# Modulation of layer 0 in float32 in four strips of the array, two parts ahead, and tokens in eight parts instead of five

## The chip, the core and the metric

The kernel runs on one core of one Trainium2 chip. The metric is the device time of one execution in microseconds; a version is judged by the median of several executions. Every time below is in microseconds unless marked ns.

## What is computed

Two blocks over 256 tokens of width 2048. The part that the change touches is the beginning of the first block, layer 0, which reads two sequences: the tokens x and a context ctx, each of 256 rows.

```python
def modulation(cond, w, b, n):
    m = jax.nn.silu(cond) @ w[:, :n * D_MODEL] + b[:n * D_MODEL]
    return jnp.split(m, n, axis=-1)

# layer 0 of first_block
sh, sc, gt = modulation(c_lat, w_ada[i], b_ada[i], 3)
u = x * (1.0 + sc) + sh
sh_c, sc_c = modulation(c_c, w_ada[i], b_ada[i], 2)
uc = ctx_s * (1.0 + sc_c) + sh_c
s_f, s_b = context_states(uc @ w_in_e[j][:, :E_STATE_COLS], ...)
y, _, _ = even_mixer(u @ w_in_e[j], s_f, s_b, ...)
x = layer_norm(alpha * x + gt * y, ln_g[i], ln_b[i])
```

The modulation is a product of two vectors (silu of c and of c_ctx, 2048 long) with the columns of w_ada: 2048 of the shift (kind 0), 2048 of the scale (kind 1) and, for x alone, 2048 of the gate. Its result is needed as one number for each of the 2048 channels. The matrix is 2048 x 6144 in float32 for a layer, 50 MB, and every element of it is used once for each of the two vectors.

The second block (a recurrent mixer, sparse attention, attention over a memory of 256 rows, an MLP) matters here only in that the keys and values of its memory are computed first of all.

## The kernel before

Everything is float32. A large product is done as three passes in a narrower format (called fp32r in the rows): both operands are split into a high and a low part, and `mm3` (L163 to L165) issues high x high, high x low and low x high into the same PSUM bank. The token side is split once, the weights as they come: `load_w` loads a tile "wr" of two k-tiles of 512 columns (512 KB, four buffers), `split_w` casts it to "wh" on ScalarE (L148) and subtracts on VectorE to get "wl" (L154, in two halves; three buffers each). A k-tile is 128 of the 2048 channels.

The work is written in order of program, and a planner (the tile framework) gives each engine its queue in an order by priority. Small streams of work that have to run beside a large one are written as generators: `bg[0]` holds one, `step(n)` advances it by n items at the places where it is called, and `drain()` runs it to its end.

The order of work around the change:

- **Memory stage** (0 to about 76 us). The memory is transposed into memT; `project` multiplies it with the 1024 columns of w_kv_cross_2, in two blocks of 512 columns with eight loads each. Beside it, one step a load, runs `ada_both(0)`, the modulation of k-tiles 0 and 1, and the norm of the memory.
- **Token stage** (to about 320 us). The loop over `PARTS`, five parts of 2, 2, 4, 4 and 4 k-tiles. A part loads its columns of x and ctx ("xn"), transposes them on TensorE (L236), applies scale and shift from mod0 and splits the result into high and low. Then, for four blocks of 512 columns of w_in_e, it loads the weights of its k-tiles and issues 24 products for each load (two k-tiles, four row blocks, three passes), into four PSUM banks. A bank is then added on VectorE to kl, vl, kc or vc (L555); in the first part it is copied by ScalarE instead.
- **Modulation for the next part** runs as `bg[0]` within the products of a part. Parts 1 and 2 get theirs from `ada_both`, two k-tiles and both kinds at a time: two loads of 256 KB into the two halves of one "wr", the same split as for any weight, and four products with c4, which holds high and low of both vectors in four columns (L349 and L350). For parts 3 and 4 kind 0 comes from `ada_block` in the same way (L327 and L328), and kind 1 from `ada_block_v` on VectorE alone: one multiply-add per k-tile and vector (L381), from the tile "ar" with two buffers. In each case a small selection product "pm" (L334, L356, L387) turns the result into one number per partition and channel, and a last VectorE instruction adds the bias into mod0. `drain()` at a part's end finishes what is left.
- **Gates and layer 1.** During the last part `bg[0]` becomes `gt_mod()`: the four gate blocks of layer 0 and the modulation of layer 1, 192 steps of one load "ar" of 256 KB and one VectorE multiply-add into "aa" (L403, L405), two steps a load of weights. The rest runs beside the stages that follow (chunked attention states up to about 865 us).

Of the kernel before, what the change touches and what calls it, by code (L numbers as in the profile page):

```python
# [8 lines left out]
F = mybir.dt.float32  # L9
# [8 lines left out]
D = 2048  # L18
# [36 lines left out]
def tile_kernel(ctx: ExitStack, tc: tile.TileContext, I: dict, out: bass.AP):  # L55
# [7 lines left out]
    PHASES = {"a": {"g": (1024, 12), "h": (512, 6), "f": (512, 6), "gt": (512, 4), "ar": (512, 2), "aa": (512, 1)},  # L63
# [245 lines left out]
    c4 = const([128, 16, 4], "c4", R)  # L309
    for a in range(2):  # L310
        col = cs[:, a * 16:(a + 1) * 16]
        S.copy(c4[:, :, 2 * a], col)
        V.tensor_tensor(c4[:, :, 2 * a + 1], col, c4[:, :, 2 * a].bitcast(F), op=AL.subtract)
    sel4 = cst[0:4, C_SEL4:C_SEL4 + 2]
# [4 lines left out]
    def ada_block(t0, nt, kind):  # L319

        n = nt * 128
        acc = pbg([4, n], "ada")
        nk = 1024 // n
        for k0 in range(0, 16, nk):
            wh, wl = load_w(ada[0], k0, nk, kind * D + t0 * 128, n)
            for q in range(nk):
                PE.matmul(acc, c4[:, k0 + q], wh[:, q], start=k0 + q == 0, stop=False)  # L327
                PE.matmul(acc, c4[:, k0 + q], wl[:, q], start=False, stop=k0 + q == 15)  # L328
            yield
        m4 = tl("h", [4, n], name="m4")  # L330
        V.tensor_copy(m4, acc)
        pm = pside([128, nt, 64, 2], name="pm")
        for q in range(nt):
            PE.matmul(pm[:, q], m4[:, q * 128:(q + 1) * 128], sel4[:, None, :].to_broadcast([4, 64, 2]), start=True, stop=True)  # L334
        for a in range(2):
            set_mod0(pm[:, :, 0, a], t0, nt, kind, a)

    def ada_both(t0):

        acc = pbg([4, 512], "ada")  # L340
        for k0 in range(0, 16, 2):
            wr = sb.tile([128, 2, 512], F, name="wr", tag="wr", bufs=4)
            for kind in range(2):
                c0 = kind * D + t0 * 128
                nc.sync.dma_start(wr[:, :, kind * 256:kind * 256 + 256],
                                  ada[0][k0 * 128:(k0 + 2) * 128, c0:c0 + 256].rearrange("(k p) m -> p k m", p=128))
# [8 lines left out]
        for q in range(4):  # L355
            PE.matmul(pm[:, q], m4[:, q * 128:(q + 1) * 128], sel4[:, None, :].to_broadcast([4, 64, 2]), start=True, stop=True)  # L356
# [1556 lines left out]
```

## Time and profile before

| what | value |
|---|---|
| median of three executions | 2561.5 us (2560.05 to 2563.88) |
| the profiled execution, its own time | 2557.92 us |
| its span on the chip | 2556.2 us |
| PE (TensorE products) busy | 2422.8 us, 95% |
| DVE (VectorE) busy | 1796.2 us, 70% |
| ACT (ScalarE) busy | 1170.2 us, 46% |
| POOL (GpSimd) busy | 172.1 us, 7% |
| granted TensorE clock, mean | 0.984 of full |
| DMA, mean | 189 GB/s; 483.11 MB in all |

The span runs from the first to the last instruction; the execution's own time contains 1.7 us more. Busy shares are means over all stages. Products on PE are pipelined and their durations overlap, so the time of a product is better read from the distance between two starts. "PEld" is the loading of weights into the array, which runs beside the products. The stationary operand of a product stands after the comma in its name, with its shape as rows x columns.

### The profile page before, as it was taken

How to read it: one execution, taken by the hardware profiler on the slowest of the kernel's cores; microseconds unless marked ns; L12 is line 12 of the kernel's file. 1: busy time of each engine (PE TensorE's matmuls, PEld its weight loads, DVE VectorE, ACT ScalarE, POOL GpSimd, SP SyncE). 2: the span in 40 equal slices, each digit the busy share in tenths (PEclk: the TensorE clock that was granted, in tenths of full speed). 3: DMA queues.
4: the chain of work that ended last, by engine and by line, in shares of the span. 5: the costliest groups of instructions: out<-in, count | busy, mean ns of one | idle time of the engine just before them, and what ended most of it. 6: DMA issues, size and time to landing. Idle time of an engine off the chain costs nothing.

```text
span 2556.2 us, 32427 instructions
## 1 busy us (share of the span) xinstructions
PE 2422.8 (95%) x11491; PEld 1928.6 (75%) x11491; DVE 1796.2 (70%) x2991; ACT 1170.2 (46%) x1560; POOL 172.1 (7%) x169
## 2 busy tenths in 40 slices
PE   8999998889989998998999999999999999999998
PEld 5667766778767776787878677787888888888886
DVE  5898657997897888967687978755655544555544
ACT  6543244444653544445642452445544433444433
POOL 0000010220230010002020120100000000000000
PEclk9999999999999999999999999999999999999999
DMA  7877547676656788755633243145466555666554
GB/s 262 276 251 225 170 153 242 218 232 228 198 183 218 233 282 288 259 182 158 198 94 110 80 136 99 63 163 192 133 189 182 186 187 187 189 184 187 201 188 154
DMA packets 267358, 483.11 MB, mean 189 GB/s; under 512 B 21137, under 2 KB 45547, under 8 KB 267195
## 3 DMA queue, kind: packets, MB, share of 16 engines
q1 hardware_dynamic: 266875, 480.60, 58.4%
q8 instruction: 90, 1.47, 0.2%
q14 instruction: 73, 0.60, 0.1%
q10 hardware_dynamic: 320, 0.44, 0.1%
HBM read 477.82 MB, written 3.15 MB: 188 GB/s over the span
## 4 chain that ended last, share of the span: by engine, by line
PE 61%; DVE 18%; DMA 11%; issue 6%; ACT 3%; POOL 1%; SPq 0%; DVEq 0%; ACTq 0%; POOLq 0%
PE acc L165 17%; PE acc L164 17%; PE acc L163 17%; DMA ar<-in_w_ada 8%; DVE wl L154 6%; DVE aa L405 3%; PE trp L236 2%; ACT wh L148 1%; DMA lnb<-in_ln_b 1%; PE pw L1457 1%; PE pz L1451 1%; DVE u L1411 1%; DVE inv L1412 1%; DMA wr<-in_w_in_e 1%; DMA wr<-in_w_in_o 0%
## 5 line engine op out<-in xcount | busy, mean ns | idle before, releaser
L148 ACT CAST wh<-wr 128x1024 fp32r<-128x1024 f32 (+2 forms) x736 | 760.3, 1038 | 991.6 <-PE acc L165 804.6
L164 PE MATMUL acc<-wl,xh 128*128 128x512 f32 (+2 forms) x2560 | 1005.5, 393 | 22.9 <-DVE wl L154 22.7
L163 PE MATMUL acc<-wh,xh 128*128 128x512 f32 (+2 forms) x2560 | 1011.8, 396 | 14.1 <-ACT xh L253 6.1
L165 PE MATMUL acc<-wh,xl 128*128 128x512 f32 (+2 forms) x2560 | 1003.5, 393 | 2.4 <-DVE xl L254 1.9
L154 DVE TENSOR_TENSOR wl<-wr,wh 128x512 fp32r<-128x512 f32 (+2 forms) x928 | 622.3, 702 | 176.8 <-ACT wh L148 176.1
L164 PEld LDWEIGHTS acc<-wl,xh 128*128 128x128 f32 x2560 | 485.1, 189 | 135.8 <-DVE wl L154 37.2
L151 DVE TENSOR_TENSOR wl<-wr,wh 128x1024 fp32r<-128x1024 f32 x272 | 333.3, 1225 | 357.4 <-ACT wh L148 355.4
L163 PEld LDWEIGHTS acc<-wh,xh 128*128 128x128 f32 x2560 | 484.6, 189 | 127.1 <-ACT wh L148 10.0
L165 PEld LDWEIGHTS acc<-wh,xl 128*128 128x128 f32 x2560 | 484.8, 189 | 106.3 <-issue 4.0
L405 DVE SCALAR_TENSOR_TENSOR aa<-ar,cs,aa 128x512 f32<-128x512 f32 x240 | 191.0, 796 | 72.8 <-DMA ar<-in_w_ada 71.5
L165 PE MATMUL acc<-wh,ucl 128*128 128x512 f32 x128 | 50.9, 398 | 0.0
L164 PE MATMUL acc<-wl,uch 128*128 128x512 f32 x128 | 50.7, 396 | 0.0
L163 PE MATMUL acc<-wh,uch 128*128 128x512 f32 x128 | 49.8, 389 | 0.0
L381 DVE SCALAR_TENSOR_TENSOR am<-ar,cs,am 128x512 f32<-128x512 f32 x60 | 42.6, 746 | 7.3 <-DMA ar<-in_w_ada 7.3
L722 PE MATMUL pp<-eq,ek 128*128 128x128 f32 x224 | 29.4, 286 | 6.1 <-DVE ek L734 6.1
L722 PEld LDWEIGHTS pp<-eq,ek 128*128 128x128 f32 x224 | 28.5, 201 | 8.4 <-issue 5.0
L1055 POOL TENSOR_TENSOR sgo<-sgo,psc 128x512 f32<-128x512 f32 x8 | 14.6, 1850 | 295.5 <-ACT sgo L1049 164.8
L350 PE MATMUL ada<-wl,c 128*4 128x512 f32 x64 | 26.0, 406 | 4.2 <-DVE wl L154 4.2
L164 PE MATMUL acc<-wl,dh 128*128 128x512 f32 x64 | 26.2, 410 | 3.8 <-DVE wl L154 3.7
L457 DVE SCALAR_TENSOR_TENSOR xl<-trp,pr,xh 128x256 fp32r<-128x256 f32 x48 | 22.3, 480 | 10.1 <-ACT xh L456 9.9
L1866 ACT ACTIVATE un<-acc,rml 128x512 f32<-128x512 f32 x32 | 22.0, 689 | 15.6 <-PE acc L165 15.6
L163 PEld LDWEIGHTS acc<-wh,uch 128*128 128x128 f32 x128 | 24.4, 191 | 5.6
(592 smaller groups left out, 2457.3 us busy)
## 6 DMA issues: line engine op xcount, KB each, us to landing
ar<-in_w_ada SPq DMA_DIRECT2D x288, 256.0 KB
wr<-in_w_in_e SPq DMA_DIRECT2D x128, 512.0 KB
wr<-in_w_up SPq DMA_DIRECT2D x128, 512.0 KB
wr<-in_w_down SPq DMA_DIRECT2D x128, 512.0 KB
wr<-in_w_in SPq DMA_DIRECT2D x80, 512.0 KB
wr<-in_w_in_o SPq DMA_DIRECT2D x64, 512.0 KB
wr<-in_w_ada SPq DMA_DIRECT2D x64, 256.0 KB
wr<-in_w_out_e SPq DMA_DIRECT2D x32, 512.0 KB
```

The costliest lines, as they stand in the source:

```text
L148: S.copy(wh, wr)
L151: engines[0].tensor_tensor(wl, wr, wh.bitcast(F), op=AL.subtract)
L154: engines[q % 2].tensor_tensor(wl[:, q], wr[:, q], wh[:, q].bitcast(F), op=AL.subtract)
L163: PE.matmul(acc, xh, wh, start=start, stop=False)
L164: PE.matmul(acc, xh, wl, start=False, stop=False)
L165: PE.matmul(acc, xl, wh, start=False, stop=stop)
L236: PE.transpose(pt[:, q, t * 128:(t + 1) * 128], src(t, kt + q), ident)
L350: PE.matmul(acc, c4[:, k0 + q], wl[:, q], start=False, stop=k0 + q == 15)
L381: V.scalar_tensor_tensor(acc[a], w[:, q], col, acc[a], op0=AL.mult, op1=AL.add)
L405: V.scalar_tensor_tensor(acc, w, cs[:, k:k + 1], acc, op0=AL.mult, op1=AL.add)
L722: PE.matmul(pp[:, h, t], kx[:, 2 * h + c, s * 128:(s + 1) * 128], qx[:, 2 * h + c, t * 128:(t + 1) * 128], start=c == 0, stop=c == 1)
L1411: V.tensor_tensor(u, inv[:, j + 1:, j:j + 1].to_broadcast([128, n, j]), inv[:, j:j + 1, :j].to_broadcast([128, n, j]), op=AL.mult)
```

## The change

Where the kernel before splits the modulation's weights and multiplies them in the narrower format, the kernel after multiplies them as they are loaded, in float32. `ada_mod(t0)` replaces `ada_both`, `ada_block` and `ada_block_v`; it does two k-tiles of channels (256 columns), both kinds. For each kind it issues four loads "wr" of four k-tiles of 256 columns (512 KB), and for each load four products with c32, which holds the two vectors repeated in 32 columns. The four products of a load go to four different strips of 32 output partitions of one PSUM bank, so that each strip sums a quarter of the k-tiles; they are issued under a raised priority. The selection "pm" now sums the four strips through a column of the constant C_ID32.

The tokens go in eight parts of two k-tiles. The modulation of parts 0 and 1 is computed in the memory stage, and part j (up to 5) computes that of part j + 2, two steps for each of its four loads. Part 6 starts `gt_mod()` with three steps a load, and part 7 goes on with it; before, the last part alone ran it, at two steps a load and eight loads.

c32 lies in a new one-buffer tile "once", which the clear of "seg" later takes over.

```diff
--- before.py
+++ after.py
@@ -60,7 +60,7 @@
 
 
     BASE = {"xt": (1024, 12), "res": (1024, 4), "bc": (512, 2), "sm": (32, 22)}
-    PHASES = {"a": {"g": (1024, 12), "h": (512, 6), "f": (512, 6), "gt": (512, 4), "ar": (512, 2), "aa": (512, 1)},
+    PHASES = {"a": {"g": (1024, 12), "h": (512, 6), "f": (512, 6), "gt": (512, 4), "ar": (512, 2), "aa": (512, 1), "once": (512, 1)},
               "b": {"yt": (1024, 8), "h": (512, 8), "f": (512, 8), "gt": (512, 4), "ar": (512, 3), "aa": (512, 1), "dt": (1024, 2)},
               "c": {"g": (1024, 11), "m": (512, 9), "l": (512, 3), "f": (512, 7), "rp": (256, 2), "c": (512, 1)},
               "d": {"u": (1024, 16), "h": (512, 12)}}
@@ -306,86 +306,37 @@
     cs = const([128, 32], "cs")
     S.activation(cs, pr1[:, :32], AF.Silu)
     load_log_exp()
-    c4 = const([128, 16, 4], "c4", R)
-    for a in range(2):
-        col = cs[:, a * 16:(a + 1) * 16]
-        S.copy(c4[:, :, 2 * a], col)
-        V.tensor_tensor(c4[:, :, 2 * a + 1], col, c4[:, :, 2 * a].bitcast(F), op=AL.subtract)
-    sel4 = cst[0:4, C_SEL4:C_SEL4 + 2]
     mod0 = const([128, 16, 2, 2], "mod0")
     mod1 = const([128, 2, 16], "mod1")
     ada = [I["w_ada"][l] for l in range(2)]
 
-    def ada_block(t0, nt, kind):
-
-        n = nt * 128
-        acc = pbg([4, n], "ada")
-        nk = 1024 // n
-        for k0 in range(0, 16, nk):
-            wh, wl = load_w(ada[0], k0, nk, kind * D + t0 * 128, n)
-            for q in range(nk):
-                PE.matmul(acc, c4[:, k0 + q], wh[:, q], start=k0 + q == 0, stop=False)
-                PE.matmul(acc, c4[:, k0 + q], wl[:, q], start=False, stop=k0 + q == 15)
-            yield
-        m4 = tl("h", [4, n], name="m4")
-        V.tensor_copy(m4, acc)
-        pm = pside([128, nt, 64, 2], name="pm")
-        for q in range(nt):
-            PE.matmul(pm[:, q], m4[:, q * 128:(q + 1) * 128], sel4[:, None, :].to_broadcast([4, 64, 2]), start=True, stop=True)
-        for a in range(2):
-            set_mod0(pm[:, :, 0, a], t0, nt, kind, a)
-
-    def ada_both(t0):
-
-        acc = pbg([4, 512], "ada")
-        for k0 in range(0, 16, 2):
-            wr = sb.tile([128, 2, 512], F, name="wr", tag="wr", bufs=4)
-            for kind in range(2):
-                c0 = kind * D + t0 * 128
-                nc.sync.dma_start(wr[:, :, kind * 256:kind * 256 + 256],
-                                  ada[0][k0 * 128:(k0 + 2) * 128, c0:c0 + 256].rearrange("(k p) m -> p k m", p=128))
-            wh, wl = split_w(wr, 2, 512)
-            for q in range(2):
-                PE.matmul(acc, c4[:, k0 + q], wh[:, q], start=k0 + q == 0, stop=False)
-                PE.matmul(acc, c4[:, k0 + q], wl[:, q], start=False, stop=k0 + q == 15)
-            yield
-        m4 = tl("h", [4, 512], name="m4")
-        V.tensor_copy(m4, acc)
+
+    c32 = tl("once", [128, 16, 32], name="c32")
+    V.tensor_copy(c32.rearrange("p k (r a) -> p r a k", a=2), cs.rearrange("p (a k) -> p a k", a=2)[:, None].to_broadcast([128, 16, 2, 16]))
+
+    def ada_mod(t0):
+
+
+        acc = pbg([128, 2, 256], "ada")
+        for kind in range(2):
+            c0 = kind * D + t0 * 128
+            for k0 in range(0, 16, 4):
+                w = sb.tile([128, 4, 256], F, name="wr", tag="wr", bufs=4)
+                nc.sync.dma_start(w, ada[0][k0 * 128:(k0 + 4) * 128, c0:c0 + 256].rearrange("(k p) m -> p k m", p=128))
+                with tc.high_priority(offset=1000):
+                    for j in range(4):
+                        PE.matmul(acc[32 * j:32 * j + 32, kind], c32[:, k0 + j], w[:, j], start=k0 == 0, stop=k0 == 12)
+                yield
+        m = tl("h", [128, 512], name="m4")
+        V.tensor_copy(m, acc.rearrange("p a b -> p (a b)"))
         pm = pside([128, 4, 64, 2], name="pm")
+        sel = cst[:, C_ID32:C_ID32 + 2]
         for q in range(4):
-            PE.matmul(pm[:, q], m4[:, q * 128:(q + 1) * 128], sel4[:, None, :].to_broadcast([4, 64, 2]), start=True, stop=True)
+            PE.matmul(pm[:, q], m[:, q * 128:(q + 1) * 128], sel[:, None, :].to_broadcast([128, 64, 2]), start=True, stop=True)
         for kind in range(2):
             b = pr1[:, 32 + kind * 16 + t0:32 + kind * 16 + t0 + 2]
-            V.scalar_tensor_tensor(mod0[:, t0:t0 + 2, kind, :], pm[:, 2 * kind:2 * kind + 2, 0, :], float(kind),
+            V.scalar_tensor_tensor(mod0[:, t0:t0 + 2, kind, :], pm[:, kind * 2:kind * 2 + 2, 0, :], float(kind),
                                    b[:, :, None].to_broadcast([128, 2, 2]), op0=AL.add, op1=AL.add)
-
-    def set_mod0(pm, t0, nt, kind, a):
-        b = pr1[:, 32 + kind * 16 + t0:32 + kind * 16 + t0 + nt]
-        V.scalar_tensor_tensor(mod0[:, t0:t0 + nt, kind, a], pm, float(kind), b, op0=AL.add, op1=AL.add)
-
-    def ada_block_v(t0, nt, kind):
-
-        n = nt * 128
-        nk = 512 // n
-        acc = [tl("gt", [128, n], name="am") for _ in range(2)]
-        for k0 in range(0, 16, nk):
-            w = tl("ar", [128, nk, n], name="ar")
-            nc.sync.dma_start(w, ada[0][k0 * 128:(k0 + nk) * 128, kind * D + t0 * 128:kind * D + (t0 + nt) * 128]
-                              .rearrange("(k p) m -> p k m", p=128))
-            for q in range(nk):
-                for a in range(2):
-                    col = cs[:, 16 * a + k0 + q:16 * a + k0 + q + 1]
-                    if k0 + q == 0:
-                        V.tensor_scalar(acc[a], w[:, q], col, None, op0=AL.mult)
-                    else:
-                        V.scalar_tensor_tensor(acc[a], w[:, q], col, acc[a], op0=AL.mult, op1=AL.add)
-            if nk > 1 or k0 % 2:
-                yield
-        for a in range(2):
-            pm = pside([128, nt, 128], name="pm")
-            for q in range(nt):
-                PE.matmul(pm[:, q], acc[a][:, q * 128:(q + 1) * 128], ones, start=True, stop=True)
-            set_mod0(pm[:, :, 0], t0, nt, kind, a)
 
     def together(*gens):
         gens = list(gens)
@@ -504,8 +455,8 @@
                     S.copy(kT_[:, q:q + 2], transpose2(lambda t, kt: kcn[t][:, kt * 128:(kt + 1) * 128], q))
                 nc.sync.dma_start(kcd, kT_)
 
-    PARTS = ((0, 2), (2, 2), (4, 4), (8, 4), (12, 4))
-    bg[0] = together(ada_both(0), mem_scale())
+    PARTS = [(t0, 2) for t0 in range(0, 16, 2)]
+    bg[0] = together(chain(ada_mod(0), ada_mod(2)), mem_scale())
     bgn_default[0] = 1
     project(memT, I["w_kv_cross_2"][0], 0, 1024, evac_kvc)
     drain()
@@ -534,9 +485,8 @@
             for q in range(0, nt, 2):
                 pt = transpose2(lambda t, kt: nat[t][:, (kt - t0) * 128:(kt - t0 + 1) * 128], t0 + q)
                 store_affine(x, t0 + q, pt, lambda kt: mod0[:, kt, 1, a:a + 1], lambda kt: mod0[:, kt, 0, a:a + 1])
-        last = j == len(PARTS) - 1
-        bg[0] = (gt_mod() if last else together(ada_block_v(*PARTS[j + 1], 1), ada_block(*PARTS[j + 1], 0)) if j > 1
-                 else chain(*[ada_both(PARTS[j + 1][0] + q) for q in range(0, PARTS[j + 1][1], 2)]))
+        if j < 7:
+            bg[0] = ada_mod(t0 + 4) if j < 6 else gt_mod()
         for cb in range(4):
             acc = [pacc() for _ in range(4)]
             for k0 in range(t0, t0 + nt, 2):
@@ -546,14 +496,14 @@
                     for q in range(2):
                         xh, xl = x.get(k0 + q, t % 2)
                         mm3(acc[t], xh, xl, wh[:, q], wl[:, q], k0 == t0 and q == 0, k0 == t0 + nt - 2 and q == 1)
-                step((2, 4, 1, 1, 2)[j])
+                step(2 if j < 6 else 3)
             for t in range(4):
                 dst = kv[("k" if cb < 2 else "v") + ("l" if t < 2 else "c")][t % 2][:, (cb % 2) * 512:(cb % 2 + 1) * 512]
                 if j == 0:
                     S.copy(dst, acc[t])
                 else:
                     V.tensor_tensor(dst, acc[t], dst, op=AL.add)
-        if not last:
+        if j < 6:
             drain()
 
     pr3 = params("pr3", [(I["conv_w"][0].rearrange("j (r p) -> (j r) p", p=128), 24),
@@ -663,7 +613,7 @@
         qT.append(to_T(lambda t, kt: qn[p, t][:, kt * 128:(kt + 1) * 128], "qT"))
 
 
-    seg = pconst([128, 512], "seg")
+    seg = tl("once", name="seg")
     G.memset(seg, 1.0)
     G.memset(seg.rearrange("p (n c) -> p n c", c=64)[:, :, 0:1], 0.0)
     onat = [None, None]
```

## Rows read from the trace of the kernel before

**Rows 1.** Busy time of each engine by stage.

```profile
core 0: us, PE busy (x) PEld busy (x) DVE busy (x) ACT busy (x) POOL busy (x), PEclk, DMA share, GB/s
25.00:76.00 51.00, 50.06 (x225) 37.31 (x224) 35.97 (x72) 28.98 (x39) 0.00 (x0) 1.00 0.85 281
76.00:120.00 44.00, 38.73 (x165) 25.28 (x164) 34.73 (x58) 27.45 (x39) 0.00 (x0) 0.92 0.81 260
120.00:165.00 45.00, 44.01 (x198) 28.39 (x197) 41.84 (x73) 23.10 (x29) 0.00 (x0) 0.96 0.85 284
165.00:320.00 155.00, 154.18 (x704) 120.47 (x703) 122.42 (x204) 47.96 (x57) 1.82 (x3) 1.00 0.64 201
450.00:865.00 415.00, 378.54 (x1772) 306.29 (x1771) 360.20 (x559) 197.59 (x229) 76.71 (x54) 0.97 0.66 217
```

**Rows 2.** Timeline (start, duration, instruction, [idle before <-releaser]), token stage's start and end.

```profile
79.83 0.45 PE L350 MATMUL ada<-wl,c 128*4 128x512 f32 x1 [2.91 <-DVE wl L154]
...
83.41 0.63 PE L163 MATMUL acc<-wh,xh 128*128 128x512 f32 x1
...
114.30 1.15 PE L356 MATMUL pm<-cst,m 4*128 4x128 f32 x8 [1.08 <-DVE m L353]
...
115.38 1.09 PE L236 MATMUL trp<-cst,xn 128*128 128x128 f32 x8
...
320.30 0.69 DVE L555 TENSOR_TENSOR vc<-acc,vc 128x512 f32<-128x512 f32 x1 [0.70 <-PE acc L165]
```

**Rows 3.** Timeline of PE where it is dense.

```profile
174.42 0.40 PE L327 MATMUL ada<-wh,c 128*4 128x512 f32 x1
...
175.35 0.39 PE L163 MATMUL acc<-wh,xh 128*128 128x512 f32 x1
...
180.85 0.40 PE L327 MATMUL ada<-wh,c 128*4 128x512 f32 x1
```

**Rows 4.** Groups of instructions (busy, mean ns, idle before), 76 to 320 us.

```profile
L154 DVE TENSOR_TENSOR wl<-wr,wh 128x512 fp32r<-128x512 f32 x146 | 93.5, 684 | 34.8 <-ACT wh L148 34.7
...
L165 PE MATMUL acc<-wh,ucl 128*128 128x512 f32 x128 | 50.9, 398 | 0.0
...
L381 DVE SCALAR_TENSOR_TENSOR am<-ar,cs,am 128x512 f32<-128x512 f32 x54 | 38.3, 745 | 2.8 <-DMA ar<-in_w_ada 2.8
...
L349 PE MATMUL ada<-wh,c 128*4 128x512 f32 x48 | 19.8, 412 | 0.0
...
L327 PE MATMUL ada<-wh,c 128*4 128x512 f32 x32 | 13.3, 416 | 0.0
...
L555 DVE TENSOR_TENSOR kc<-acc,kc 128x512 f32<-128x512 f32 x16 | 11.0, 687 | 1.9 <-PE acc L165 1.9
```

**Rows 5.** Waits (who, for what: total, times, longest), 76 to 320 us.

```profile
PE ada L350 <- DVE wl L154: 4.2, 3, 2.9
...
DVE am L381 <- DMA ar<-in_w_ada: 2.8, 4, 1.0
...
ACT wh L148 <- DMA wr<-in_w_in_e: 2.7, 2, 2.5
```

**Rows 6.** Timeline of PE, a float32 run of 8 output partitions among products.

```profile
1291.26 0.40 PE L164 MATMUL acc<-wl,xh 128*128 128x512 f32 x1
1291.59 1.03 PE L1308 MATMUL pn<-ksq,cst 128*8 128x256 f32 x4
1292.55 0.50 PE L165 MATMUL acc<-wh,xl 128*128 128x512 f32 x1
1292.89 0.39 PE L163 MATMUL acc<-wh,xh 128*128 128x512 f32 x1
```

**Rows 7.** Timeline of PE, float32 products into two halves of the output partitions.

```profile
1405.23 0.66 PE L1482 MATMUL pr__11340<-sr,ga 128*64 128x128 f32 x8
1405.82 0.50 PE L164 MATMUL acc<-wl,xh 128*128 128x512 f32 x1
```

**Rows 8.** Waits, 334 to 865 us.

```profile
DVE aa L405 <- DMA ar<-in_w_ada: 56.6, 60, 3.7
...
PE acc L164 <- DVE wl L154: 17.6, 14, 4.4
```

## The prediction, made before the kernel after had run

> **What bounds the kernel now.** I read first the busy time of each engine by stage [rows 1]. The two stages that the change touches are the memory stage (keys and values of the memory, to about 76 us) and the token stage (76 to 320 us, where the last addition into vc stands [rows 2]). In both TensorE is busy almost throughout, with VectorE close behind up to 165 us, and DMA at 260 to 284 GB/s until then and 201 GB/s after.
>
> A busy matmul row is pipelined, so its 0.4 us says little; what counts is the distance between starts [rows 3]. Four modulation products start at 174.42 and the next product at 175.35: 0.93 / 4 = 0.233 us each. The 24 token products from 175.35 to 180.85 give 5.50 / 24 = 0.229 us each. The grouped lines then give the work [rows 4]: there are 768 token products (six rows of 128; one stands), 160 modulation products between 76 and 320 us (48 each of lines 349 and 350, 32 each of 327 and 328) and nine small selections "pm" of 8 records, 1.08 us each (114.30 to 115.38 [rows 2]).
>
> Content of the token stage: 768 x 0.229 + 160 x 0.233 + 9 x 1.08 = 175.9 + 37.3 + 9.7 = 222.9 us, out of 244.6. The other 21.7 us are the transposes of x and ctx (kept as they are) and stalls. By the stages [rows 1], 165 to 320 us holds 704 records in 155 us, 0.220 each, and can't be denser; the stretch from 76 to 165 holds 363 records in 89 us, 0.245 each, although some are short ones. Its content is 192 x 0.229 + 96 x 0.233 + 3 x 1.08 = 69.6 us and two parts' transposes (16 records a part, 8 in 1.09 us [rows 2], 4.4 us), so about 15 us of the stall lies there. Rows show the places: TensorE waits 2.91 us for VectorE's residue of a modulation load, the first token product is at 83.41, and 1.08 us pass before "pm" [rows 2]; the waits name VectorE's split of modulation weights [rows 5]. So the bound is TensorE's queue, plus stalls at the starts of the first parts, where the modulation for a part is finished only as the part begins.
>
> **The change, part by part.** *Modulation products.* Removed: 192 products at 0.233 us, 32 of them in the memory stage (7.5 us) and 160 in the token stage (37.3 us). Added: 64 loads, each with four float32 products of 256 columns, into four different strips of 32 output partitions. The trace has no four strips, but two nearby cases. One strip alone [rows 6]: between the products at 1291.26 and 1292.89 stand one product and a float32 run of 4 records (two to an instruction) of 256 columns. 1.63 less two products (0.46) leaves 1.17 us. A record carries float32 in two passes, so its 256 columns take what 512 take in a product, 0.22; 4 x 0.22 = 0.88, and 0.29 is the price of leaving the full array and coming back. Two strips [rows 7]: 8 records of 128 columns (0.11 each, so 0.88 in a row) begin at 1405.23, and the next product begins at 1405.82, 0.59 later, a return included. They ran two at a time. A load's group of 8 records therefore costs 2 x 0.22 + 0.29 + 0.02 = 0.75 us if all four strips run together, 4 x 0.22 + 0.29 = 1.17 if two do, and 8 x 0.22 + 0.29 = 2.05 if none do. I take 0.75: strips did overlap fully where there were two. Memory stage: 16 groups, 12.0 - 7.5 = **+4.5 us**. Token stage: 48 groups, 36.0 - 37.3 = **-1.3 us**. So the change buys TensorE nothing by its arithmetic.
>
> *Selections.* Ten "pm" become eight, two in the memory stage where there was one: **+1.1** there, 6 instead of 9 behind it, **-3.2 us**.
>
> *The splits.* 48 modulation loads no longer need a cast on ScalarE and two subtractions on VectorE (0.684 us each [rows 4]): 96 x 0.684 = 65.7 us, and some 64 multiply-adds of the VectorE variant at 0.709 (38.3 / 54): 45.4 us. Eight parts instead of five add 48 additions into kl, vl, kc, vc at 0.687: 33.0 us. Net VectorE -78 us. Off the path where TensorE is dense: I book it at nothing there. The additions cost nothing as long as a PSUM bank is emptied before its turn comes round, one column block (5.5 us) later; four take 2.7 us and a split 1.4, so that cover has 1.4 us left. Without it each part would lose up to 1.4 us.
>
> *Two parts ahead.* No part waits for its own modulation any more: no residue of a modulation load, no copy and "pm" on the path at a part's start. Of the 15 us I take **-12** back; bounds 0 (something else arrives last) and -15.
>
> *New wait.* TensorE now waits for the load itself, in its own queue, raised over the products. Queued behind the wait are all token products; nobody else can run meanwhile. Today engines with slack wait for loads in this stage only 2.8 us (4 times) and 2.7 us (2 times) [rows 5]; later, where VectorE takes loads from two buffers as they land, 60 waits cost 56.6 us, 0.94 each [rows 8]. For 48 groups the bounds are 0 and 48 x 0.94 = 45 us. I take **+4**, near the rows of this stage: the four load buffers and the bytes of a block are what the first two parts have now. On SP's queue 48 issues fall away, but a modulation load's buffer is now freed by TensorE, so the token loads behind it wait for that too.
>
> *Gates pulled forward.* Gate and layer-1 loads start two parts before the end at three steps a block: 24 steps instead of 16 before the states. Eight steps (0.79 us and 0.94 us of waiting each) leave a stretch where VectorE is busy 360 of 415 us [rows 1] and TensorE waits 17.6 us for it [rows 8]. Bounds 0 and 8 x 1.73 = -14; **-3**, as TensorE has other work there. The clear of seg moves behind the last group on POOL, with two stages to spare: nothing.
>
> **The sum.** +4.5 - 1.3 + 1.1 - 3.2 - 12 + 4 - 3 = -9.9, say -10 us. The span of 2556.2 becomes 2546; the profiled run was 2557.9 and the median of the runs 2561.5, so the median should be 2551.5 us (-0.4%).
>
> **Rivals.** *A: TensorE stalls on the loads (slower).* Each group is placed as early as its data were expected; if half of the 48 come late by 0.94, the wait costs 23 us instead of 4, and -10 becomes +9 to +12: 2572 us. It decides from about 14 us of stall, 0.3 us a group. For it: the rate needed, three loads of 512 KB per block of 5.5 + 1.5 = 7 us, is 225 GB/s, and TensorE holds two of three. Against it: the chip moved 284 GB/s between 120 and 165 us, and the loads were hardly waited for [rows 1, 5].
>
> *B: the strips don't run four at a time.* Two at a time: 64 x 0.42 = +27, 2578 us; one at a time: 64 x 1.30 = +83, 2635 us. Against: the pairs of [rows 7]. For: four moving streams at once are nowhere in the trace.
>
> *C: they run together, but not at the full rate.* If the overlap gets only three quarters of the way from two strips at a time (0.88 us for a group's records) to four (0.44), the records take 0.55: 64 x 0.11 = +7, 2558.5 us, the same as before. The row of two strips [rows 7] speaks for the full rate. The Trainium skill ("TensorE: Matmul & The Clock Gate", Part 3: Packing small matmuls) gives 2.38 for three column tiles, which is 0.79 of full rate and would make a group's records 0.55. No run here shows four.
>
> *D: the memory stage is held by DMA.* It gets 4.2 MB more, and 51 us of it ran at 281 GB/s already [rows 1]. Of its 16.8 MB of weights, 60 us at that rate, about 5 more would show beyond the 5.6 booked: 2556.5 us, within or just over the bound of no change. What speaks against: today part of the DMA time before 76 us goes to loads for the token stage, which then come later.
>
> **Chances.** Forecast 0.50; A 0.22; B 0.11 (two at a time 0.08); C 0.05; D 0.12. A measurement of this kernel can tell about 0.2%, 5 us, from no change. Faster takes the forecast: 0.50; same C and D: 0.17; slower A and B: 0.33. The range must reach A and the two-at-a-time case: up to 2580. Down, the waits at nothing, stalls at -15 and the gates at -9 give -23; not all come together: 2538. It leaves out most of one at a time, and the tails. The forecast's own range is 2540 to 2557.
>
> **What would show it.** Groups: 8 records within 0.75 us, starts of four strips within some tens of ns; 1.17 or 2.05 says B. The memory stage ends at about 82 us instead of 76, the last addition into vc comes at about 314 instead of 320. Waits of TensorE on the modulation load: 4 us in total if I am right, over 20 if A is. First token product with no gap behind the memory's last. Gates: first "pbg" of the gates before the states begin, before the last part's products are through, at some 300 us. Wrong altogether would be a DMA stall outside of both stages, or additions that hold back PSUM banks: TensorE waiting for VectorE's additions.

## The result: 0.7% slower

The kernel after takes 2577.7 us (median of four executions, 2575.9 to 2585.6), the kernel before beside it 2562.7: a ratio of 1.0071 with a 95% interval of 1.0050 to 1.0091. The forecast was 2551.5, faster; the time lies in its range, on the other side. The profiled execution took 2575.9 us, its span is 2574.0, 17.8 more than before.

The stages of the kernel after, to be held against [rows 1] (same columns):

```profile
25.00:76.00 51.00, 48.79 (x287) 32.78 (x287) 20.84 (x46) 16.72 (x21) 0.00 (x0) 1.00 0.92 295
76.00:120.00 44.00, 41.14 (x254) 25.95 (x252) 12.47 (x24) 19.21 (x30) 0.00 (x0) 0.96 0.89 279
120.00:165.00 45.00, 38.32 (x228) 24.58 (x228) 26.39 (x43) 8.34 (x12) 0.00 (x0) 1.00 0.81 260
165.00:320.00 155.00, 139.76 (x732) 101.51 (x731) 105.85 (x173) 32.20 (x41) 2.29 (x5) 0.99 0.64 201
320.00:338.50 18.50, 18.50 (x86) 15.24 (x86) 16.69 (x28) 3.72 (x4) 0.00 (x0) 1.00 0.65 199
```

VectorE fell as forecast (34.7 to 12.5 us busy between 76 and 120 us, 41.8 to 26.4 between 120 and 165). But TensorE, which had been busy for 154 of the 155 us from 165 to 320, is now busy for 140 of them: the stage that could not be denser has gaps, and it ends later.

From here on the token stage is counted from the start of the last copy into kvc (the end of the memory stage) to the start of the last addition into vc. Its row, first of the kernel before, then of the kernel after:

```profile
75.90:320.30 244.40, 237.32 (x1067) 174.44 (x1066) 199.00 (x334) 98.62 (x122) 1.82 (x3) 0.98 0.71 227
```

```profile
79.20:338.30 259.10, 234.52 (x1280) 164.96 (x1281) 161.21 (x265) 61.75 (x85) 2.29 (x5) 0.99 0.71 224
```

The memory stage is longer by 3.3 us, the token stage by 14.7; behind it both kernels need the same, 2556.2 - 320.3 = 2235.9 and 2574.0 - 338.3 = 2235.7 us. So the whole loss stands in the two stages that were changed, and what it consists of is in the waits of the kernel after from 76 to 338.5 us (who, for what: total, times, longest), to be held against [rows 5]:

```profile
PE ada L328 <- DMA wr<-in_w_ada: 13.7, 16, 2.0
...
PE acc L163 <- ACT xh L253: 8.5, 5, 2.2
...
PE pm L335 <- DVE m L331: 1.6, 1, 1.6
```

In [rows 5] TensorE had waited 4.2 us for a modulation load's split and for no load at all. Now it waits 13.7 us for loads, in 16 of 48 groups, and 8.5 us for the affine step at the starts of parts. Both can be seen in one stretch, a part's start and the first group after it:

```profile
154.64 1.04 PE L236 MATMUL trp<-cst,xn 128*128 128x128 f32 x8
...
155.28 0.99 DVE L251 TENSOR_SCALAR full<-trp,mod 128x256 f32<-128x256 f32 x2
155.85 1.02 ACT L252 ACTIVATE full<-trp,mod 128x256 f32<-128x256 f32 x2 [1.58 <-DVE full L251]
...
156.77 0.61 ACT L253 CAST xh<-full 128x512 fp32r<-128x512 f32 x1
...
157.43 0.50 PE L163 MATMUL acc<-wh,xh 128*128 128x512 f32 x1 [1.76 <-ACT xh L253]
...
161.57 0.64 PE L328 MATMUL ada<-wr,c 128*32 128x256 f32 x8 [1.55 <-DMA wr<-in_w_ada]
```

The transposes end at 155.7, then TensorE has nothing until VectorE, ScalarE and the cast have passed the tile on, 1.76 us. At 160.02, two and a half us later, it stands before a group whose load is not there, 1.55 us, with token products queued behind.

A group without a wait, to be held against the bounds of [rows 6] and [rows 7]:

```profile
36.61 0.39 PE L165 MATMUL acc<-wh,xl 128*128 128x512 f32 x1
36.93 0.64 PE L328 MATMUL ada<-wr,c 128*32 128x256 f32 x8
37.50 0.50 PE L163 MATMUL acc<-wh,xh 128*128 128x512 f32 x1
37.84 0.39 PE L164 MATMUL acc<-wl,xh 128*128 128x512 f32 x1
```

From 36.61 to 37.84 there are two products and a group: 1.23 - 2 x 0.229 = 0.77 us for the group. The other groups without a wait between two token products come out the same (median 0.78 in the token stage).

### The profile page after: what moved, and what is told of

It is laid out like the page before. It is cut to its first block, busy times and chain, and to the rows that moved or that the text cites. A ratio compares the mean times of both kernels' runs of the same rounds, so it can differ in the third digit from the quotient of the medians.

```text
span 2574.0 us, 32630 instructions
## 1 busy us (share of the span) xinstructions
PE 2420.5 (94%) x11795; PEld 1920.7 (75%) x11795; DVE 1732.6 (67%) x2880; ACT 1123.6 (44%) x1510; POOL 170.0 (7%) x169
## 4 chain that ended last, share of the span: by engine, by line
PE 51%; DVE 11%; DMA 3%; issue 2%; ACT 2%; POOL 0%; SPq 0%; ACTq 0%; DVEq 0%; POOLq 0%
PE acc L163 15%; PE acc L165 15%; PE acc L164 15%; DVE wl L154 3%; DMA ar<-in_w_ada 2%; PE trp L236 1%; DVE aa L356 1%; PE pw L1407 1%; PE pz L1401 1%; DVE u L1361 1%; DVE inv L1362 1%; DMA lnb<-in_ln_b 1%; ACT wh L148 1%; DMA wr<-in_w_in_o 0%; PE psr L1339 0%
## 5 line engine op out<-in xcount | busy, mean ns | idle before, releaser
L148 ACT CAST wh<-wr 128x1024 fp32r<-128x1024 f32 (+1 forms) x688 | 712.6, 1037 | 1035.7 <-PE acc L165 861.1
L163 PE MATMUL acc<-wh,xh 128*128 128x512 f32 (+2 forms) x2560 | 1015.8, 397 | 19.7 <-ACT xh L253 14.9
L154 DVE TENSOR_TENSOR wl<-wr,wh 128x512 fp32r<-128x512 f32 (+2 forms) x832 | 557.5, 699 | 197.4 <-ACT wh L148 197.0
L328 PE MATMUL ada<-wr,c 128*32 128x256 f32 x512 | 41.6, 396 | 16.3 <-DMA wr<-in_w_ada 15.8
L328 PEld LDWEIGHTS ada<-wr,c 128*32 128x32 f32 x512 | 10.2, 108 | 39.7 <-DMA wr<-in_w_ada 25.2
L505 DVE TENSOR_TENSOR vc<-acc,vc 128x512 f32<-128x512 f32 x28 | 19.3, 691 | 21.2 <-PE acc L165 21.1
L505 DVE TENSOR_TENSOR kc<-acc,kc 128x512 f32<-128x512 f32 x28 | 19.3, 691 | 17.4 <-PE acc L165 17.3
L165 PEld LDWEIGHTS acc<-wh,ucl 128*128 128x128 f32 x128 | 24.1, 188 | 8.0 <-issue 2.9
```

Source lines behind the costliest of these rows:

```text
L148: S.copy(wh, wr)
L154: engines[q % 2].tensor_tensor(wl[:, q], wr[:, q], wh[:, q].bitcast(F), op=AL.subtract)
L163: PE.matmul(acc, xh, wh, start=start, stop=False)
L165: PE.matmul(acc, xl, wh, start=False, stop=stop)
L328: PE.matmul(acc[32 * j:32 * j + 32, kind], c32[:, k0 + j], w[:, j], start=k0 == 0, stop=k0 == 12)
L505: V.tensor_tensor(dst, acc[t], dst, op=AL.add)
```

## The experiments

All are edits of the kernel after, if nothing else is said. Ratios are to the kernel before, run beside each on the same chip. The numbers of stages come from one profiled execution each; what lies behind the token stage varied between 2230 and 2241 us in kernels that differ only ahead of it (2250 and 2247 in two), so a stage is read from its own row and the time from the ratio.

The texts written before the runs name three theories of the loss. W: TensorE waits in its own queue for modulation loads. P: the starts of the eight short parts. G: the gates' loads, which come earlier now, delay the others. Later ones split W by its reason: ring (the shared buffers wr), rate (of DMA) and place (where a group stands in TensorE's queue). Where they give 15.6 or 15.9 us of waits in front of groups for the kernel after, the waits view of its token stage has 13.7.

### What the loads cost: no_mod_loads

```diff
-                w = sb.tile([128, 4, 256], F, name="wr", tag="wr", bufs=4)
-                nc.sync.dma_start(w, ada[0][k0 * 128:(k0 + 4) * 128, c0:c0 + 256].rearrange("(k p) m -> p k m", p=128))
...
-                        PE.matmul(acc[32 * j:32 * j + 32, kind], c32[:, k0 + j], w[:, j], start=k0 == 0, stop=k0 == 12)
+                        PE.matmul(acc[32 * j:32 * j + 32, kind], c32[:, k0 + j], cst[:, j * 128:j * 128 + 256], start=k0 == 0, stop=k0 == 12)
```

> The kernel after with the 64 modulation loads of layer 0 left out: the groups multiply columns of a constant that lies in SBUF (so the modulation itself is not computed). Groups, selections, parts and gates stay. W: the waits in front of groups go, 15.6 us in the token stage and 2.4 us in the memory stage, and the products' waits for late weights with them: 2553 to 2562 us. P: the 8.5 us at the starts of parts stay, and no more than 5 us go: 2572 to 2578. If DMA alone held the memory stage, that stage would end at least 5 us sooner than 79.2.

Measured: ratio 0.9952 (0.9937 to 0.9968). Its token stage and its waits there:

```profile
72.60:304.30 231.70, 218.93 (x1283) 172.84 (x1283) 147.34 (x247) 60.78 (x83) 2.35 (x5) 0.99 0.38 116
```

```profile
PE acc L163 <- ACT xh L253: 10.4, 5, 2.2
PE ada L326 <- DVE m L329: 1.8, 2, 1.3
```

259.1 to 231.7: the token stage is 27.4 us shorter, the memory stage 79.2 - 72.6 = 6.6, and the time is under what even W expected. Not all of this is waiting for loads. With nothing to wait for, the planner puts the eight groups of a part in one run:

```profile
111.21 0.62 PE L165 MATMUL acc<-wh,xl 128*128 128x512 f32 x2
111.77 3.66 PE L326 MATMUL ada<-cst,c 128*32 128x256 f32 x64
115.36 0.50 PE L163 MATMUL acc<-wh,xh 128*128 128x512 f32 x1
115.69 0.39 PE L164 MATMUL acc<-wl,xh 128*128 128x512 f32 x1
```

From 111.21 to 115.69 there are three products and eight groups: 4.48 - 3 x 0.229 = 3.79 us, 0.47 a group where one alone costs 0.77. Over 48 groups that is 14 us, and 13.7 are the waits: the edit took away both, so the loads themselves cost about half of the 27. The groups, placed singly, cost 48 x 0.77 = 37.0 us, as much as the products that they replaced (37.3), so they alone don't make the kernel slow. The wait at the starts of parts stays (10.4 us).

### The raised priority: no_priority

```diff
-                with tc.high_priority(offset=1000):
+                if True:
```

> The kernel after, without the raised priority of the four modulation products of a load. Theory W (TensorE waits in its own queue for modulation loads, 15.6 us in front of the 48 groups of the token stage of the kernel after): the groups fall to later places in TensorE's queue, where their loads have landed, and most of the 15.6 us go: 2563 to 2570 us against 2577.7. Rival P (the starts of the eight short parts cost it, 8.5 us between transposes and first products): no change, 2575 to 2580. Rival G (the gates' loads, pulled forward to 134 us, take DMA and VectorE): no change either.

Measured: ratio 1.0065 (1.0044 to 1.0087). Waits in the token stage, and two of its groups:

```profile
PE pm L335 <- DVE m L331: 15.4, 7, 3.7
```

```profile
184.77 1.07 PE L328 MATMUL ada<-wr,c 128*32 128x256 f32 x16
197.86 1.07 PE L328 MATMUL ada<-wr,c 128*32 128x256 f32 x16
```

No wait for a load is left, as W expected; the groups come in pairs (16 records). But the last ones stand at the end of a part, and TensorE waits for the copy of their result before the selection: 15.4 us in 7 waits. The memory stage ends at 85.9, 6.7 later, the token stage takes 245.7; this execution, at 2563.7 us, is the fastest of six with a median of 2574.0, so its stages look better than the ratio. W missed the time. P and G, which expected no change, have the time but not the reason: one wait went and another took its place.

### The gates: gates_late

```diff
-        if j < 7:
+        if j != 6:
             bg[0] = ada_mod(t0 + 4) if j < 6 else gt_mod()
...
-                step(2 if j < 6 else 3)
+                step(2)
```

> The kernel after with the gates' and layer 1's stream started only in the last part at two steps a load of weights, as in the kernel before. G: with no gate loads between 134 and 264 us the waits of the token stage shrink by 6 us or more: below 2572 us. W and P: the time stays within 3 us of 2577.7, since the gates' earlier end bought nothing after 338 us in the kernel after, and 26 gate loads were only 6.8 MB. If pulling the gates forward was worth the 3 us of the prediction, this kernel is 3 us slower, 2581.

Measured: ratio 1.0110 (1.0076 to 1.0144). The token stage is the same, 259.3 us (80.0 to 339.3), so rival G falls: the gates' loads are not what delays the others. What lies behind the stage took 2580.9 - 339.3 = 2241.6 us, 5.9 more than after. That points the same way as the 3 us that the prediction gave to the gates, but the ratios' intervals overlap, and that stretch varies by as much.

### The starts of parts: prep_early and old_products_eight_parts

`prepare` holds the loads, transposes and affine step of a part, as they stood in the loop:

```diff
-    for j, (t0, nt) in enumerate(PARTS):
+    def prepare(t0, nt):
...
+
+    prepare(*PARTS[0])
+    for j, (t0, nt) in enumerate(PARTS):
...
         for cb in range(4):
+            if cb == 2 and j < 7:
+                prepare(*PARTS[j + 1])
```

> The kernel after with loads, transposes and affine step of a part written into the middle of the part before (ahead of its third column block). P: the gaps between the transposes of a part and its first product (7 of 1.2 us more than the dense distance, 8.5 us together) go: 2568 to 2571 us. W: TensorE then arrives at the next modulation load sooner and waits there; no more than 3 us are gained, 2574 to 2578.

Measured: ratio 1.0035 (1.0011 to 1.0059). Token stage and waits:

```profile
78.40:326.30 247.90, 234.49 (x1284) 166.55 (x1284) 154.27 (x255) 61.86 (x85) 2.22 (x5) 0.97 0.70 222
```

```profile
PE ada L328 <- DMA wr<-in_w_ada: 11.7, 10, 2.7
...
PE acc L163 <- ACT xh L253: 1.8, 1, 1.8
```

P holds: the token stage is 11.2 us shorter. Some 9 of them are the starts of parts (waits of 8.5 and 1.6 us after, 1.8 here), 2 come from the waits for loads, of which 11.7 stay. The kernel before with eight parts, the other half of P:

```diff
-    PARTS = ((0, 2), (2, 2), (4, 4), (8, 4), (12, 4))
+    PARTS = [(t0, 2) for t0 in range(0, 16, 2)]
...
+        bg[0] = gt_mod() if last else ada_both(PARTS[j + 1][0])
...
-                step((2, 4, 1, 1, 2)[j])
+                step(2)
```

> The kernel before with eight parts of two k-tiles, each with the modulation of the next part by the old products (all by the variant with both kinds), gates in the last part. P: three more part starts, each with a gap of 1.2 us or a wait for the modulation, and 78 us more of VectorE work than in the kernel after (additions and splits), so 5 us slower than before or more: 2567 to 2575 us against 2562.7. W: the parts as such cost nothing, within 3 us of the kernel before.

Measured: ratio 1.0170 (1.0131 to 1.0209), worse than either theory. Token stage and waits:

```profile
74.30:348.40 274.10, 255.20 (x1121) 179.04 (x1120) 219.35 (x363) 114.42 (x139) 1.58 (x3) 0.98 0.66 209
```

```profile
PE pm L356 <- DVE m L353: 8.5, 7, 1.2
...
PE ada L350 <- DVE wl L154: 5.1, 2, 4.1
PE acc L163 <- ACT xh L253: 4.1, 7, 1.0
```

Of the 29.7 us more than before, 64 x 0.233 = 14.9 are products that VectorE had done before and that have nothing to do with the parts. Most of the rest is starts: selection, split and affine step wait in a row, seven times. So eight parts by themselves cost this kernel some 15 us in the token stage; by the token stages (274.1 to 259.1) float32 groups two parts ahead give back 15 of the 30. The ratio is worse than the two first stages: behind them this kernel takes 2598.4 - 348.4 = 2250.0 us, 14 more than before. Its last part is shorter and starts the gates with fewer steps, which may be the reason; no run separates it.

### The products without the parts: groups_in_five_parts

The kernel before with `ada_mod` in place of the three old forms (and so two steps a load in the third and fourth part), without the eight parts, the two parts of lead and the earlier gates:

```diff
...
+    bg[0] = together(ada_mod(0), mem_scale())
...
+        bg[0] = gt_mod() if last else chain(*[ada_mod(PARTS[j + 1][0] + q) for q in range(0, PARTS[j + 1][1], 2)])
...
-                step((2, 4, 1, 1, 2)[j])
+                step((2, 4, 2, 2, 2)[j])
```

> The kernel before with its five parts, its one part of lead and its late gates, but with the modulation of layer 0 by the float32 products in four strips under raised priority, as in the kernel after. Theory W: TensorE waits for its loads in front of groups here too; 56 groups behind the memory stage, some 0.3 us each, 15 to 20 us, while the memory stage is 3 us shorter than in the kernel after and only part starts of five parts are paid: 2568 to 2578 us against 2562.7 of the kernel before. Rival P (the eight parts are what costs): no slower than the kernel before, 2558 to 2563.

Measured: ratio 1.0007 (0.9989 to 1.0026).

```profile
81.30:332.90 251.60, 235.73 (x1319) 165.28 (x1318) 127.93 (x213) 61.05 (x83) 2.35 (x5) 0.99 0.74 234
```

```profile
PE ada L327 <- DMA wr<-in_w_ada: 12.4, 17, 1.3
...
PE acc L163 <- ACT xh L253: 2.8, 4, 1.8
```

W's waits are here too (12.4 us), yet the ratio is that of the kernel before: by the ratio, the new products with their waits are worth as much as the old ones with theirs, W, which expected a loss, missed, and what makes the kernel after slower is what the eight parts and their lead add. The rows don't bear this out in full. The token stage is 7.2 us longer than before and the memory stage ends 5.4 later; the profiled execution makes up for it behind them, with 2562.6 - 332.9 = 2229.7 us against 2235.9. So of the 14.7 us that the token stage of the kernel after lost, up to half may come from the groups and their waits; the ratio and the stage rows disagree on it.

### Buffers of their own: own_buffers, own_ring and three combinations

A first idea of where W's waits come from was the shared ring of four wr. In own_buffers a load is two halves in gt:

```diff
-                w = sb.tile([128, 4, 256], F, name="wr", tag="wr", bufs=4)
+                w = [tl("gt", [128, 2, 256], name="wm") for _ in range(2)]
...
```

> The kernel after, with the modulation weights in tiles of their own: two halves of 256 KB for a load, in the four buffers of gt, which the gates need only later; the four wr are left to the token weights. Same bytes, products and parts. If the waits of theory W come from the shared ring of four wr (a load is issued only when TensorE has run an earlier group), most of the 15.6 us in front of groups go, and 8 us or more with them: 2563 to 2570 us on the scale on which the kernel after has 2577.7. If they come from the rate of DMA as such (the stretches ran at 213 to 277 GB/s), the time stays within 4 us of the kernel after.

Measured: ratio 1.0201 (1.0158 to 1.0244), token stage 279.0 us (87.3 to 366.3). A miss, and the timeline says why:

```profile
150.04 0.63 PE L329 MATMUL ada<-wm,c 128*32 128x256 f32 x4
150.60 0.50 PE L163 MATMUL acc<-wh,xh 128*128 128x512 f32 x1
...
151.51 0.62 PE L329 MATMUL ada<-wm,c 128*32 128x256 f32 x4
152.06 0.50 PE L163 MATMUL acc<-wh,xh 128*128 128x512 f32 x1
```

With two loads for a group the planner tore it into halves of two strips, and half a group costs as much as a whole one (0.56 us to the next product, against 0.57 for eight records above). The waits for loads were small (2.2 us in 4), but nothing follows from that for the ring. The combination with prep_early has the same fault (ratio 1.0152):

> own_buffers and prep_early together: modulation weights in tiles of their own, and the affine step of a part in the middle of the part before. prep_early alone took 11.2 us off the token stage (259.1 to 247.9). If W's waits come from the shared ring, both gains add: token stage below 240 us, and the time below the kernel before, 2553 to 2560 where that has 2562.7. If DMA's rate holds the stage, it stays near 248 us and the time near prep_early's (1.0035 of the kernel before).

own_ring keeps a load whole:

```diff
-"gt": (512, 4), "ar": (512, 2), "aa": (512, 1), "once": (512, 1)},
+"gt": (1024, 2), "ar": (512, 2), "aa": (512, 1), "once": (512, 1)},
...
-                w = sb.tile([128, 4, 256], F, name="wr", tag="wr", bufs=4)
+                w = tl("gt", [128, 4, 256], name="wm")
...
```

> As own_buffers, but a modulation load stays one tile of 512 KB, so that the four products of a group stay together (in own_buffers the halves tore the groups apart, 80 entries from the token products instead of 43): two tiles of 512 KB take the memory of gt, whose four gates then lie in pairs. Theory W with the shared ring as its cause: the waits in front of groups (15.9 us in the token stage of the kernel after, 5.3 in own_buffers) fall below 6 us and the token stage from 259 to about 250 us, 2566 to 2571 us. If DMA's rate or the latency of a load sets them, they stay above 12 us and the time within 4 us of the kernel after.

Measured: ratio 1.0080 (1.0049 to 1.0110), token stage 260.3 us.

```profile
PE ada L328 <- DMA wm<-in_w_ada: 12.5, 11, 2.5
PE acc L163 <- ACT xh L253: 11.4, 6, 2.2
```

The ring falls as the cause in the kernel after: the waits for loads are what they were. With prep_early it is the same (ratio 1.0026, 1.0006 to 1.0045; waits for loads 14.1 us). In five parts the waits fell from 12.4 to 7.1 us and the token stage from 251.6 to 246.6, so there the ring may have a share; the ratio, 0.9994 (0.9980 to 1.0008), can't be told from that of groups_in_five_parts:

> own_ring together with prep_early. Ring: token stage 238 to 242 us (247.9 in prep_early, less the 8 to 10 us of waits in front of groups) and the time at or below the kernel before, ratio 0.998 to 1.001. Otherwise as prep_early, ratio 1.0035, token stage 248 us.

> groups_in_five_parts (ratio 1.0007, token stage 251.6 us, 12.0 us of waits in front of groups) with modulation loads in two tiles of their own. Ring: the waits shrink by 6 to 8 us, ratio 0.997 to 0.999. Otherwise as groups_in_five_parts.

### The place in TensorE's queue: behind_half, behind_block and two combinations

```diff
...
+                        done = mm3(acc[t], xh, xl, wh[:, q], wl[:, q], k0 == t0 and q == 0, k0 == t0 + nt - 2 and q == 1)
+                    if j < 6 and t % 2:
+                        with tc.issue_after(done.ins):
+                            step(1)
...
```

> The kernel after, with each group of four products tied behind the token products of half a block: after the products of x in its block the first, after those of ctx the second (TensorE's order alone is changed; loads, buffers and bytes are the same). Theory place: the groups stand in TensorE's queue where the planner expected their load, 0.3 to 2 us before it lands; tied to a later place, the waits in front of groups fall from 15.9 to below 4 us and the token stage from 259 to 245 to 250 us, ratio 1.002 to 1.004. Rival rate: three loads of 512 KB a block can't come faster than they do; the waits then move to the token weights (TensorE waiting for the split's wh or wl) and the token stage stays between 255 and 262 us, ratio 1.006 to 1.008.

Measured: ratio 1.0075 (1.0042 to 1.0108), token stage 257.3 us (79.6 to 336.9).

```profile
PE acc L163 <- ACT xh L253: 15.2, 7, 2.9
...
PE pm L335 <- DVE m L331: 7.0, 6, 2.1
```

The waits for loads are gone, not smaller: no such row of TensorE's products is left, with the same loads, buffers and bytes. So they came from the place, and no wait for the token weights' split took their turn, as rate had expected. But the time did not move, and stands where rate had it: the last group of a part now ends it, and copy, selection, transposes and affine step follow one another while TensorE waits 15.2 + 7.0 = 22.2 us, as many as the 13.7 + 8.5 + 1.6 = 23.8 of the kernel after. Both groups at the end of a block (behind_block):

```diff
...
+                if j < 6:
+                    with tc.issue_after(done.ins):
+                        step(2)
...
```

> As behind_half, but both groups of a block are tied behind the block's last product. Place: no waits in front of groups either, and one return to the full array a block less (0.3 us each, 24 of them in the token stage), but the buffers of two modulation loads are held to the end of a block and the next come together: token stage 243 to 252 us. Rate: 255 us or more.

Measured: ratio 1.0065 (1.0048 to 1.0083), token stage 252.9 us, between the two forecasts. The waits for loads are gone here too, the starts have 11.7 + 5.7 us, and the products wait 4.2 + 1.6 us for the split of token weights, so a little of what rate expected is in this one.

behind_half with the prepare of prep_early has next to nothing left to wait for:

> behind_half together with prep_early (token stage 247.9 us, of it 11.5 us of waits in front of groups). Place: token stage 236 to 240 us, ratio 0.997 to 1.000. Rate: 246 to 250 us, ratio 1.003.

Measured: ratio 0.9978 (0.9962 to 0.9993).

```profile
82.00:316.20 234.20, 231.39 (x1282) 162.87 (x1281) 153.16 (x256) 61.49 (x85) 2.22 (x5) 0.99 0.75 235
```

```profile
PE acc L163 <- ACT xh L253: 2.1, 1, 2.1
...
PE pm L335 <- DVE m L331: 0.6, 1, 0.6
```

The token stage is shorter than in the kernel before (244.4), as place forecast. DMA moves more here (235 GB/s over the stage, against 224 after), so its rate did not hold the kernel after. With buffers of their own on top:

> behind_half_prep_early with the modulation loads in two tiles of their own. If, once the groups are placed later, it is the shared ring that holds the token loads back, this one is better by 3 us or more in the token stage; if not, it equals behind_half_prep_early within 2 us.

Measured: ratio 0.9969 (0.9954 to 0.9983), 2553.3 us beside 2559.4: token stage 232.8 us against 234.2, the memory stage ends at 76.9 instead of 82.0. This is the lowest ratio of all, 0.3% under the kernel before and 1% under that of the kernel after; its interval overlaps that of behind_half_prep_early. The ring makes no difference in the token stage; the 5 us in the memory stage, where no group was tied to a place, were not foreseen, and one execution doesn't settle them.

## Why the prediction was wrong

Two terms failed: the -12 us for two parts ahead, whose reason was incomplete, and the +4 us for the new wait, whose size was too small. The rest of the sum came out near its booking, but for the gates, which are not settled.

- **Modulation products: right.** 0.75 us a group were booked and 0.77 measured. Four strips run at once: half a group costs as much as a whole. Rivals B and C fall. The Trainium skill ("TensorE: Matmul & The Clock Gate", Part 3: Packing small matmuls) gives a speedup of 2.38 for three column tiles. This trace shows more for four: the third and fourth strip cost 0.01 us on top of two.
- **Memory stage: right in sign.** 5.6 us were booked, 3.3 measured. TensorE waited 2.1 us for modulation loads in it, but rival D's 5 us beyond the booking did not come, although the stretch from 25 to 76 us ran at 295 GB/s.
- **Splits: VectorE's load fell as booked**, and no row shows anything that ended sooner for it.
- **Two parts ahead: the step that failed.** -12 us were booked out of 15 us of stall between 76 and 165 us, with the reason that no part would wait for its own modulation. It waits for none, but between the transposes and the first product stands the affine step on VectorE and ScalarE, and with eight short parts TensorE has little to lay over it. In the kernel before modulation products lay in that gap; at this start the first product followed without a wait:

```profile
216.26 1.53 PE L236 MATMUL trp<-cst,xn 128*128 128x128 f32 x12
217.55 0.48 PE L327 MATMUL ada<-wh,c 128*4 128x512 f32 x1
...
218.89 0.40 PE L328 MATMUL ada<-wl,c 128*4 128x512 f32 x1
219.12 0.50 PE L163 MATMUL acc<-wh,xh 128*128 128x512 f32 x1
```

  "Kept as they are" was said of the transposes, and their consequence was not priced: 8.5 us of waits in the kernel after. The gain was also too large. By [rows 1] TensorE is idle for 89 - 38.73 - 44.01 = 6.3 us between 76 and 165 us, not 15, and its waits for the modulation in the token stage are the 4.2 us of [rows 5] and 1.9 more:

```profile
PE pm L356 <- DVE m L353: 1.9, 2, 1.1
```

  Some 5 of the other 9 us, an estimate, are the clock, which [rows 1] has at 0.92 and 0.96 there: from 80.1 to 86.8 and from 158.6 to 161.9 us it was granted at the lower of its two levels (0.50 of full, 1.2 GHz), and products start 0.43 us apart instead of 0.229 for these 10 us.
- **New wait: mis-sized.** +4 us were booked, with bounds of 0 and 45; the row says 13.7. Rival A had the mechanism: a group placed where its load was expected, with the token products queued behind it. It had 23 us, half of the groups late by 0.94 each; 16 of 48 were, by 0.86. What it gave as support, the rate and the buffers held by TensorE, is not the reason: behind_half_prep_early has neither fewer loads nor more buffers and no such waits. Its time of 2572 is near the 2577.7 measured by some luck, as it has the waits too long, the starts of parts at nothing and all of the 12 us regained. That the planner put the groups where it expected their loads fits this, and is argued, not shown.
- **What it adds up to.** The groups gave -0.3 us (48 x 0.77 - 37.3), the selections -3.2, taken as booked, and the old waits -6.1; 13.7, 8.5 and 1.6 us of waits are new. That makes +14.2, and the stage grew by 14.7.
- **Gates: not settled.** -3 us were booked, the stretch behind the token stage is 0.2 us shorter. gates_late points the same way as the booking, within its noise.
- Of the signs that were named, the first product without a gap behind the memory's last did not come, and the waits on the modulation load over which A was to be judged (4 or over 20) came out between.

What stays open is the share of each wait in the 0.7%. Taken away one at a time, the load waits cost nothing (behind_half) and the starts half of it (prep_early); taken away together they are worth 25 us of the token stage, 259.1 to 234.2.

## What to carry to other kernels

A wait taken off an in-order queue goes to the next thing that is late in the same queue: price the row behind it before booking the gain, here the 1.8 us from transposes to first product, times the number of parts. An instruction that waits for a load belongs in the queue behind work that is ready, not where the load is expected. And when two waits stand in for each other, only the experiment that removes both shows what they are worth. An edit that takes a wait away can also let the planner put the work in another order, as in no_mod_loads: read what else moved before its whole gain is put down to the wait.

## What was not expected of the hardware

- Leaving the full array and coming back costs the same for two strips and for four: a group of eight records in four strips takes 0.57 us to the next product, four records in two strips 0.56. Groups in a row share it: 16 records have 1.07 us of row, where eight have 0.64, and eight groups in a row cost 0.47 us each, one alone 0.77.
- Some of the gaps were followed by a lower clock. After the wait of 2.00 us that ended at 170.04 in the kernel after, the granted clock fell to the lower level, and products start 0.43 us apart:

```profile
170.40:173.70 3.30, 3.30 (x15) 2.29 (x8) 1.08 (x2) 0.00 (x0) 0.00 (x0) 0.50 0.54 185
```

  The gap of 1.76 us before 84.61 was followed by such a stretch too (85.0 to 88.3), the one of 1.76 before 157.43 was not. Over the token stage the kernel after has less of it than the kernel before (0.99 of full against 0.98), so the clock is not what made it slower.
